# First half's output projection moved between the second half's receptances and values in a two-layer RWKV-7 and S5 trunk

## The chip, the cores and the metric

One core of a Trainium2 chip runs the whole kernel. The metric is the time of one execution in device microseconds (us): the median of three runs before the change is 2767.67 us (2766.5 to 2772.65). A difference under 0.2%, some 5.5 us, is called no change.

## The reference

The input x is 1024 steps of 1024 channels. Layer 0 is RWKV-7 time mixing, layer 1 a diagonal state-space mixer (S5), each followed by a squared-ReLU MLP, and after each of the four parts comes `x <- LayerNorm(sqrt(2) * x + f(x))`. The change lies in layer 0:

```python
r = xr @ wr; k = xk @ wk; v = xv @ wv          # xr, xk, xv: x mixed with its last step
w_pre = w0 + tanh(xw @ w1) @ w2                # decay
a = sigmoid(a0 + (xa @ a1) @ a2); g = sigmoid(xg @ g1) @ g2
def step(state, inp):                          # 16 heads of 64, 1024 steps in sequence
    sa = einsum('bhvk,bhk->bhv', state, a_t)
    state = state * w_t + sa * b_t + v_t * k_t
    return state, einsum('bhvk,bhk->bhv', state, r_t)
o = group_norm(o) * lnx_g + lnx_b + bonus
return (o * g) @ wo
```

## The kernel before

All operands are float32. A dense product of 128 output channels by 512 steps is made of three TensorE matmuls for each 128 input channels: both operands are split into a high part (rounded by ScalarE, `whi`, `oAh`) and the rest (subtracted by VectorE, `wlo`, `oAl`), and high x high, high x low and low x high are summed in one PSUM tile `d` (`mm3`, `dense`, L175). So a projection of 1024 channels on half the sequence is 8 tiles of 24 matmuls.

The sequence is worked in two halves of 512 steps. `rwkv_proj(H)` computes receptances, keys, values, rates and gates of half H and stores them in DRAM. The recurrence then runs in 8 **units** m = 0 to 7, each 256 steps by 8 heads: units 0 to 3 belong to the first half, units 4 to 7 to the second. Even and odd units carry the states of different heads. For a unit, `elem` forms the decayed vectors, `amat` (L550 on) the chunk matrices (`AT`: products within 64-step chunks), `invert` the triangular inverses `XT` by some 60 short VectorE instructions in sequence, and `chain` walks four 64-step chunks: products pR, pX, pU, pO of 8 heads (L672, L677, L682, L691 and L693), each waiting for a copy of the one before. `gnorm` normalises and writes the unit's y to DRAM.

`core()` lists these pieces with a priority (`rank`): a scheduler places the instructions of all engines by it, lowest number first where they are ready. What it makes is a fixed order for each engine, each worked strictly in that order; DMAs are issued by SyncE's queue in such an order too. The dense products have high numbers and fill the time that the chains leave. `rwkv_proj(1)` is listed at unit 3 (`PB`), all of it with rank 100000. At unit 5 (`W0B`) come `wo(0)`, the output projection of the first half (rank 99000), and its LayerNorm (rank -1). `wo` loads y, makes its operands, and adds each product to sqrt(2) x in a tile `hA`. The MLP's products follow: `up` (relu, square, split into `qbuf`) and `down`.

Two pools matter. Tag "xs" holds 8 tiles: the mixed input's x of the second half until the last mix (that for the values) has read it, then `hA`. Tag "q" has one buffer, which is held in turn by `stash`, by the chunk matrices `AT2` of units 1, 3 and 5 (all other units have their own tile `AT`), and then by the MLP's `qbuf`:

```python
if D.m in (1, 3, 5):
    at = ap.tile(shp, F32, tag="q", name="AT2", bufs=1)
else:
    at = kp.tile(shp, F32, tag="AT", name="AT", bufs=1)
```

Of the kernel before, what the change touches and what calls it, by code (L numbers as in the profile page):

```python
# [8 lines left out]
F32 = mybir.dt.float32  # L9
# [9 lines left out]
HT = 512  # L19
# [13 lines left out]
TB = 2  # L33
LN8R = 400000
MIXR = 100
W0B = 5
ARB = 5
GB = (2, 3, 4)
GV = True
# [31 lines left out]
def trunk(ctx, tc, A):  # L71
# [13 lines left out]
    @contextmanager  # L85
    def rank(base):

        keep = tc.cur_priority
        tc.cur_priority = base
        yield  # L90
        tc.cur_priority = keep
# [137 lines left out]
    def rwkv_proj(H):  # L229
# [196 lines left out]
        else:  # L426
# [8 lines left out]
            for n in range(KT):  # L435
                square("wr", "r", xm, n)


        xv = list(mixes(3))
        for cb in range(4):  # L440
# [260 lines left out]
    def gnorm(D, half):  # L701

        def gwt(shape, name):
            if D.m < 4:
                return tp.tile(shape, F32, tag="la", name=name, bufs=2)
            return kp.tile(shape, F32, tag=GWT, name=name, bufs=1)

        q, o, vsa = D.q, D.o[half], D.vsa[half]
        t0 = D.t0 + half * 128
        og = o.rearrange("p c i v -> p (c i) v")  # L710
        bc = [128, 8, 64]
        sm = kp.tile([128, 8], F32, tag="sm", name="sm", bufs=2)
        V.tensor_reduce(sm, og, axis=AX.X, op=ALU.add)
        V.tensor_scalar(sm, sm, 1.0 / 64, None, op0=ALU.mult)
        (G if GNG[0] else V).tensor_sub(og, og, sm.unsqueeze(2).broadcast_to(bc))
        sq = gwt([128, 8, 64], "osq")
        S.activation(sq, og, AF.Square)
        vr = kp.tile([128, 8], F32, tag="sm", name="vr", bufs=2)
        V.tensor_reduce(vr, sq, axis=AX.X, op=ALU.add)
        V.tensor_scalar(vr, vr, 1.0 / 64, GN_EPS, op0=ALU.mult, op1=ALU.add)  # L720
        G.tensor_tensor(vr, vr, mhalf[:, 0:8], op=ALU.pow)
        (G if GNG[1] else V).tensor_mul(og, og, vr.unsqueeze(2).broadcast_to(bc))
        vt = gwt([128, 2, NP, 64], "vt")
        if half == 0:
            D.lg = kp.tile([128, 2, 256], F32, tag="lg", name="lg", bufs=LGB)
            for h in range(2):
                for j in range(2):
                    fs = slice(q * 512 + h * 256, q * 512 + h * 256 + 256)
                    SP.dma_start(D.lg[64 * (1 - h) : 64 * (1 - h) + 64, j], A["lnx"][j : j + 1, fs].broadcast_to([64, 256]))
        lg = D.lg  # L730
        for h in range(2):
            hs = slice(64 * (1 - h), 64 * (1 - h) + 64)
            G.tensor_mul(vt[hs], vsa[hs, :, h],
                         D.bo[hs, 2 * half : 2 * half + 2].unsqueeze(3).broadcast_to([64, 2, NP, 64]))
        o2 = o.rearrange("p c i v -> p c (i v)")
        v2 = vt.rearrange("p c i v -> p c (i v)")
        G.tensor_add(v2, v2, lg[:, 1:2].broadcast_to([128, 2, 256]))
        G.tensor_mul(o2, o2, lg[:, 0:1].broadcast_to([128, 2, 256]))
        G.tensor_add(o, o, vt)
        rows = slice(q * 512, q * 512 + 512)  # L740
        gt = kp.tile([128, NP, 128], F32, tag="gt", name="gt", bufs=GTB)
        SP.dma_start(gt, scr["g"][rows, t0 : t0 + 128].rearrange("(i p) t -> p i t", p=128))

        p = pc.tile([128, HT], F32, tag="c", name="py").rearrange("p (u h c l) -> p u h c l", u=2, h=2, c=2)
        for u in range(2):
            for c in range(2):
                PE.transpose(p[:, u, :, c], o[:, c, 2 * u : 2 * u + 2].rearrange("p i v -> p (i v)"), ident)
        V.tensor_mul(gt, gt, p.rearrange("p u h c l -> p (u h) (c l)"))
        SP.dma_start(scr["y"][rows, t0 : t0 + 128].rearrange("(i p) t -> p i t", p=128), gt)

    def run(gen):
        for _ in gen:
            pass

    first_out = []

    def core():

        pg = rwkv_proj(0)
        next(pg)  # L760
        bulk.clear()
        with rank(3000):
            cur = elem(0)
        with rank(5000):
            amat(cur)
            invert(cur)
        with rank(100000):
            run(pg)
        last = None
        for m in range(8):  # L770
            if m == PB:
                with rank(100000):
                    run(rwkv_proj(1))
            if m == W0B:

                with rank(WO0R):
                    first_out.append(wo(0))
                with rank(LN1R):
                    first_out.append(layer_norm(first_out[0], 0, 0))
            base = m * 10000  # L780
            with rank(base + RK[0]):
                kbtrans(cur)
            nxt = None
            if m < 7:
                with rank(base + RK[1]):
                    nxt = elem(m + 1)
            if last and m in GB:
                with rank(base + RK[2]):
                    gnorm(last, 1)
            with rank(base):  # L790
                chain(cur, 0)
            if last and m not in GB:
                with rank(base + RK[2]):
                    gnorm(last, 1)
            if nxt and m < 6:
                with rank(base + RK[3]):
                    amat(nxt)
            with rank(base + RK[4]):
                chain(cur, 1)
            with rank(base + RK[5]):  # L800
                gnorm(cur, 0)
            if nxt:
                with rank(base + RK[6]):
                    if m == 6:
                        amat(nxt)
                    invert(nxt)
            last, cur = cur, nxt
        with rank(base + 8000):
            gnorm(last, 1)


    def htile(H):
# [2 lines left out]
        return sp.tile([128, HT], F32, tag="hB", name="hB", bufs=8)  # L815

    def layer_norm(h, gi, H, split_out=True):
        g, b = f"g{gi}", f"b{gi}"

        def lt(name, tag="la"):  # L820
            return tp.tile([128, HT], F32, tag=tag, name=name, bufs=2)

        def plt(name):
            return pl.tile([128, HT], F32, tag="l", name=name)

        a, b2 = lt("sa"), lt("sb")
        G.tensor_add(a, h[0], h[1])
        G.tensor_add(a, a, h[2])
        V.tensor_add(b2, h[3], h[4])
        for t in h[5:7]:  # L830
            V.tensor_add(b2, b2, t)
        V.tensor_add(a, a, b2)
        pm = plt("pm")
        PE.matmul(pm, ones_c, a, start=True, stop=False)
        PE.matmul(pm, ones_c, h[7], start=False, stop=True)
        for t in h:
            V.tensor_sub(t, t, pm)
        sa = [lt("sq0"), lt("sq1")]
        for k, t in enumerate(h):
            if k < 2:  # L840
                S.activation(sa[k], t, AF.Square)
            else:
                q = lt("sq", "m")
                S.activation(q, t, AF.Square)
                (G if k % 2 else V).tensor_add(sa[k % 2], sa[k % 2], q)
        pq = plt("pq")
        for t in range(4):
            for j in range(2):
                PE.matmul(pq[:, t : t + 1], sa[j][:, t * 128 : (t + 1) * 128], ones_c[:, 0:1], start=j == 0, stop=j == 1)  # L849
        rs = tp.tile([128, 4], F32, tag="rs", name="rs")  # L850
        V.tensor_scalar(rs, pq[:, 0:4], LN_EPS, None, op0=ALU.add)
        G.tensor_tensor(rs, rs, mhalf[:, 0:4], op=ALU.pow)
        rb = lt("rb").rearrange("p (t n) -> p t n", t=4)
        S.copy(rb, rs.unsqueeze(2).broadcast_to([128, 4, 128]))
        pr = plt("pr")
        for t in range(4):
            PE.transpose(pr[:, t * 128 : (t + 1) * 128], rb[:, t], ident)
        ops = []
        for k, t in enumerate(h):
            V.tensor_mul(t, t, pr)  # L860
            S.activation(t, t, AF.Identity, bias=vec(b, k), scale=vec(g, k))
            if split_out:
                ops.append(operand(t, H, G if k in LNG else V))
        return ops

    def last_norm(h, gi, c):
# [49 lines left out]
            ys.append(operand(y, H))  # L916
        return ys

    def wo(H):
        t0 = H * HT  # L920
        ys = yload(H)
        hs = []
        for n in range(KT):
            p = psd()
            dense(p, wload(A["wo"][n], KT, 128), ys)
            h = htile(H)
            SP.dma_start(h, A["xT"][n * 128 : (n + 1) * 128, t0 : t0 + HT])
            V.scalar_tensor_tensor(h, h, ALPHA, p, op0=ALU.mult, op1=ALU.add)
            hs.append(h)
        return hs  # L930
# [309 lines left out]
        for k in range(KT):  # L1240
            SP.dma_start(A["out"][k * 128 : (k + 1) * 128, H * HT : (H + 1) * HT], h[k])

    core()
    kctx.close()
    sp = ctx.enter_context(tc.tile_pool(name="sp", bufs=1))

# [1 line left out]
    bw = sp.tile([128, 4, 32, 2], F32, name="bw")  # L1248
    qbuf = ap.tile([128, 2 * KB2, 2, HT], F32R, tag="q", name="qbuf", bufs=1)
    tc.cur_priority = 200000  # L1250
    hA, xo = first_out
    ma = mlp(0, 0, hA, xo)
    for _ in range(INS1):
        next(ma)
# [110 lines left out]
```

## Time and profile before

| | |
|---|---|
| median of three runs | 2767.67 us |
| the profiled execution | 2764.91 us, of which its span 2763.2 us |
| busy share of the span: TensorE (PE), VectorE (DVE), ScalarE (ACT), GpSimd (POOL) | 94%, 68%, 40%, 26% |
| mean granted TensorE clock | 0.958 of full speed |
| moved by DMA | 318.63 MB, mean 115 GB/s |

The profile gives, for each engine, how long it worked, and, for idle time before an instruction, what ended it. A matmul's recorded time overlaps its neighbours', so the rate is read from the distance between starts. A float32 product of the chains shows as two records for each matmul. PEclk is the mean granted clock of TensorE as a share of 2.4 GHz; its two levels are 1.2 and 2.4 GHz.

### The profile page before, as it was taken

The numbers are of one execution on the slowest core, as the hardware profiler recorded it, in microseconds if no ns is written. First come the engines' busy times: TensorE is split into PE (matmuls) and PEld (weight loads), VectorE is DVE, ScalarE is ACT, GpSimd is POOL, SyncE is SP. The second block draws the span as 40 slices with busy tenths as digits, with TensorE's granted clock in tenths as the row PEclk, the third lists the DMA queues.
The fourth block names the chain that finished last, engine by engine and source line by source line (L and its number), as shares of the span: only waits on it lengthen the run. The fifth ranks groups of instructions, "written<-read, shape, count | busy, mean of one in ns | idle before, by whom it ended". The sixth has DMA issues, their size and how long they took to land.

```text
span 2763.2 us, 43707 instructions
## 1 busy us (share of the span) xinstructions
PE 2604.9 (94%) x16582; PEld 2096.5 (76%) x16582; DVE 1884.5 (68%) x3242; ACT 1109.5 (40%) x1952; POOL 719.6 (26%) x601
## 2 busy tenths in 40 slices
PE   7889989889899999989999999999999999999997
PEld 5779767678677877767776788778778887788886
DVE  7487788587787777998658554574765546755556
ACT  5445454544443333334432332344323323533333
POOL 5331664450352303233122001121220101210101
PEclk9989969889889999999999999999999999999998
DMA  3543443344222323555332633223343322333333
GB/s 115 184 147 112 139 162 102 109 138 135 77 81 81 100 85 124 154 145 159 96 122 99 203 96 98 89 88 102 117 160 112 99 96 84 119 96 97 98 95 100
DMA packets 200083, 318.63 MB, mean 115 GB/s; under 512 B 19520, under 2 KB 73920, under 8 KB 199872
## 3 DMA queue, kind: packets, MB, share of 16 engines
q1 hardware_dynamic: 199872, 315.83, 36.6%
q8 instruction: 131, 2.15, 0.3%
q14 instruction: 80, 0.66, 0.1%
HBM read 265.42 MB, written 50.33 MB: 114 GB/s over the span
## 4 chain that ended last, share of the span: by engine, by line
PE 45%; DVE 5%; issue 2%; POOL 1%; DMA 1%; ACT 0%; ACTq 0%; DVEq 0%; POOLq 0%
PE d L175 40%; PE py L1219 1%; PE py L1224 1%; DVE wlo L147 1%; PE pu L152 1%; DVE t L1187 1%; PE pbu L1175 1%; DVE hA L960 0%; DVE hB L960 0%; DVE t L1185 0%; POOL rl L944 0%; PE pq L849 0%; DMA wraw<-in_mw_dram 0%; PE pu L1164 0%; DVE qbuf L147 0%
## 5 line engine op out<-in xcount | busy, mean ns | idle before, releaser
L147 DVE TENSOR_TENSOR wlo<-wraw,whi 128x512 fp32r<-128x512 f32 x720 | 535.6, 745 | 443.7 <-ACT whi L146 424.8
L146 ACT CAST whi<-wraw 128x512 fp32r<-128x512 f32 x720 | 445.7, 620 | 975.4 <-PE d L175 637.2
L175 PE MATMUL d<-qbuf,whi 128*128 128x512 f32 (+1 forms) x2112 | 655.6, 393 | 20.9 <-DVE hA L960 9.4
L175 PEld LDWEIGHTS d<-qbuf,whi 128*128 128x128 f32 x2112 | 390.3, 190 | 117.7 <-DVE hA L960 17.0
L944 POOL TENSOR_TENSOR rl<-rl 128x512 f32<-128x512 f32 x128 | 158.6, 1239 | 1058.4 <-ACT rl L943 1018.1
L175 PE MATMUL d<-qbuf,wlo 128*128 128x512 f32 (+1 forms) x1056 | 409.3, 390 | 8.2 <-DVE wlo L147 8.0
L175 PE MATMUL d<-oAh,whi 128*128 128x512 f32 (+1 forms) x960 | 387.8, 408 | 9.6 <-ACT ev L404 7.2
L175 PE MATMUL d<-oAh,wlo 128*128 128x512 f32 (+1 forms) x960 | 387.2, 406 | 5.3 <-DVE wlo L147 5.1
L175 PE MATMUL d<-oAl,whi 128*128 128x512 f32 (+1 forms) x960 | 385.5, 404 | 1.4 <-DVE oAl L147 1.4
L175 PE MATMUL d<-oBh,wlo 128*128 128x512 f32 x704 | 278.3, 396 | 1.4 <-DVE wlo L147 1.4
L175 PE MATMUL d<-oBh,whi 128*128 128x512 f32 x704 | 278.8, 396 | 0.0
L175 PE MATMUL d<-oBl,whi 128*128 128x512 f32 x704 | 276.1, 392 | 0.0
L175 PEld LDWEIGHTS d<-qbuf,wlo 128*128 128x128 f32 x1056 | 200.6, 190 | 52.8 <-DVE wlo L147 11.7
L175 PEld LDWEIGHTS d<-oAh,whi 128*128 128x128 f32 (+1 forms) x960 | 185.1, 194 | 54.2 <-ACT ev L404 9.2
L175 PEld LDWEIGHTS d<-oAh,wlo 128*128 128x128 f32 (+1 forms) x960 | 184.9, 193 | 49.1 <-DVE wlo L147 8.6
L175 PEld LDWEIGHTS d<-oAl,whi 128*128 128x128 f32 (+1 forms) x960 | 184.8, 193 | 40.6 <-DVE oAl L147 2.1
L960 DVE TENSOR_TENSOR hB<-hB,d 128x512 f32<-128x512 f32 (+1 forms) x256 | 165.2, 650 | 68.9 <-PE d L175 65.8
L960 DVE TENSOR_TENSOR hA<-hA,d 128x512 f32<-128x512 f32 x240 | 162.5, 683 | 54.5 <-PE d L175 52.5
L175 PEld LDWEIGHTS d<-oBh,wlo 128*128 128x128 f32 x704 | 132.5, 188 | 33.8 <-DVE wlo L147 2.0
L175 PEld LDWEIGHTS d<-oBl,whi 128*128 128x128 f32 x704 | 132.7, 188 | 29.4 <-issue 0.5
L175 PEld LDWEIGHTS d<-oBh,whi 128*128 128x128 f32 x704 | 132.7, 189 | 29.1 <-issue 1.5
L147 DVE TENSOR_TENSOR qbuf<-rl,qbuf 128x512 fp32r<-128x512 f32 x128 | 99.0, 774 | 70.3 <-ACT qbuf L146 69.8
(371 smaller groups left out, 3877.1 us busy)
## 6 DMA issues: line engine op xcount, KB each, us to landing
wraw<-in_mw_dram SPq DMA_DIRECT2D x520, 256.0 KB, 2.7
wraw<-in_glu_dram SPq DMA_DIRECT2D x64, 256.0 KB, 2.6
wraw<-in_wk_dram SPq DMA_DIRECT2D x32, 256.0 KB, 3.1
wraw<-in_wr_dram SPq DMA_DIRECT2D x32, 256.0 KB, 3.1
wraw<-in_wv_dram SPq DMA_DIRECT2D x32, 256.0 KB, 3.4
yl<-s_y SPq DMA_DIRECT2D x32, 256.0 KB, 3.1
wraw<-in_wo_dram SPq DMA_DIRECT2D x32, 256.0 KB, 2.8
tb<-tB SPq DMA_DIRECT2D x16, 512.0 KB, 4.9
```

The lines of the kernel that those rows point to most:

```text
L146: S.copy(hi, src)
L147: (e or V).tensor_sub(lo, src, hi.bitcast(F32))
L152: PE.matmul(out, x, idt, start=True, stop=True)
L175: bulk.append((PE.matmul(p, w, x, **kw).ins, x.shape[-1]))
L944: G.tensor_mul(r, r, r)
L960: V.tensor_add(z, z, p)
L1175: PE.matmul(p[qs, g2, ri], tb[:, g2, ri, qs], u[:, 2 * g2 + par], start=True, stop=True)
L1187: e.tensor_mul(t2[:, :, ri], x[:, :, 1 - ri], bw[:, l, g0:g1, ri : ri + 1].broadcast_to([128, g1 - g0, n]))
L1219: PE.matmul(p[64 * j : 64 * j + 64, g2], ug[f][:, 2 * g2 + par], tv[:, par, g2], start=g2 == 0, stop=False, skip_group_check=True)
L1224: PE.matmul(p[64 * j : 64 * j + 64, g2], hb[qs, 4 * f + g2, ri, 0:NSC], tcm[qs, g2, ri], start=False, stop=ri == 1, skip_group_check=True)
```

## The change

`rwkv_proj(1)` stops after the receptances. `wo(0)` is listed there, at unit 4, and puts its sums in a new tile `pre` of tag "q", which thus lies between the chunk matrices of unit 3 and those of unit 5. Then the values of the second half are listed, then the LayerNorm, cut in `ln_stats` and `ln_apply`; the latter writes its result to fresh `hA` tiles of tag "xs".

```diff
             for n in range(KT):
                 square("wr", "r", xm, n)
+        if H == 1:
+            yield
         xv = list(mixes(3))
...
             if m == PB:
+                pg = rwkv_proj(1)
                 with rank(100000):
-                    run(rwkv_proj(1))
-            if m == W0B:
-
-                with rank(WO0R):
-                    first_out.append(wo(0))
-                with rank(LN1R):
-                    first_out.append(layer_norm(first_out[0], 0, 0))
+                    next(pg)
...
+            if m == 4:
+
+                pre = ap.tile([128, KT, HT], F32, tag="q", name="pre", bufs=1)
+                with rank(WO0R):
+                    hA = wo(0, pre)
+                with rank(100000):
+                    run(pg)
+                with rank(LNR):
+                    xo = ln_apply(hA, ln_stats(hA), 0, 0, fresh=True)
...
+    def ln_apply(h, pr, gi, H, split_out=True, fresh=False):
+        g, b = f"g{gi}", f"b{gi}"
         ops = []
         for k, t in enumerate(h):
             V.tensor_mul(t, t, pr)
-            S.activation(t, t, AF.Identity, bias=vec(b, k), scale=vec(g, k))
+            h[k] = htile(H) if fresh else t
+            S.activation(h[k], t, AF.Identity, bias=vec(b, k), scale=vec(g, k))
...
-    def wo(H):
+    def wo(H, room=None):
...
-            h = htile(H)
+            h = htile(H) if room is None else room[:, n]
```

What that does to the order of instructions is seen at three places. First, SyncE's queue at the end of the receptances (`in_wr`, `in_wo`, `in_wv` are the weights of receptances, output projection and values; `hA` and `pre` receive x; `yl` is a row of y). Before:

```order
L163 DMA wraw<-in_wv_dram 128x512
L927 DMA hA<-in_xT_dram 128x512
L485 DMA ldr<-s_r 128x2x256
L927 DMA hA<-in_xT_dram 128x512 x2
L163 DMA wraw<-in_wv_dram 128x512
L927 DMA hA<-in_xT_dram 128x512
L485 DMA ldsg<-s_sg 128x2x256
L485 DMA lda<-s_a 128x2x256
L927 DMA hA<-in_xT_dram 128x512
L163 DMA wraw<-in_wv_dram 128x512
```

and after it:

```order
L938 DMA pre<-in_xT_dram 128x512 x7
L487 DMA ldk<-s_k 128x2x256
L938 DMA pre<-in_xT_dram 128x512
L751 DMA s_y<-gt 128x4x128
L163 DMA wraw<-in_wo_dram 128x512
L365 DMA s_r<-ev 128x512
L163 DMA wraw<-in_wo_dram 128x512
```

The loads of x for the output projection stood between the weights of the values; now they stand together ahead of the first weights of the output projection, which follow the receptances directly.

Second, VectorE's order around the chunk matrices of unit 5, which are `AT_6976` before and `AT_7453` after (an `AT` with no number is an even unit's). Before, they are written during the values' projection:

```order
L570 TENSOR_TENSOR AT_6976<-pA,amask 128x2x256
L608 TENSOR_TENSOR x_6530<-xa,x_6530 128x96
L570 TENSOR_TENSOR AT_6976<-pA,amask 128x2x256
L610 TENSOR_TENSOR x_6530<-x_6530 128x8x12
L608 TENSOR_TENSOR x_6530<-xa,x_6530 128x84
```

and now:

```order
L857 TENSOR_SCALAR rs<-pq 128x4
L147 TENSOR_TENSOR wlo<-wraw,whi 128x512
L870 TENSOR_TENSOR pre<-pre,pr 128x512 x8
L147 TENSOR_TENSOR wlo<-wraw,whi 128x512
L680 COPY vsa<-pX 64x256
L572 TENSOR_TENSOR AT_7453<-pA,amask 128x2x256 x2
L147 TENSOR_TENSOR wlo<-wraw,whi 128x512 x2
L687 TENSOR_TENSOR st<-pU,st 128x256
```

They come behind the LayerNorm's last multiplications, in the time of unit 4's chain, and no longer among the steps of unit 4's inverse.

Third, TensorE's order at the start of unit 5's chain (`pT` are transposes for that chain, `pv` the last products of its inverse, `pm` the LayerNorm's mean, `pb` and `pss` products of unit 6's `elem`). Before:

```order
L580 MATMUL pT<-ident,KB 128x128 x4
L175 MATMUL d<-oAh,whi 128x512
L175 MATMUL d<-oAl,whi 128x512
L175 MATMUL d<-oAh,wlo 128x512
L175 MATMUL d<-oAh,whi 128x512
L175 MATMUL d<-oAl,whi 128x512
L175 MATMUL d<-oAh,wlo 128x512
L672 MATMUL pR<-vsa,AT_6976 64x64 x8
L544 MATMUL pb<-rksel,kf 64x1 x2
L834 MATMUL pm<-sa,ones_c 128x512
L544 MATMUL pb<-rksel,kf 64x1 x12
L835 MATMUL pm<-hA,ones_c 128x512
```

and now:

```order
L749 MATMUL py<-ident,o 128x2x64 x4
L582 MATMUL pT<-ident,KB 128x128 x4
L623 MATMUL pv_7717<-x_7644,AT_7453 32x32 x32
L582 MATMUL pT<-ident,KB 128x128 x8
L631 MATMUL pv_7717<-XT,x_7644 32x32 x32
L582 MATMUL pT<-ident,KB 128x128 x4
L546 MATMUL pb<-rksel,kf 64x1 x7
L674 MATMUL pR<-vsa,AT_7453 64x64 x8
L546 MATMUL pb<-rksel,kf 64x1 x9
L509 MATMUL pss<-hsel,sq 128x2 x4
L679 MATMUL pX<-o,XT 64x64 x8
```

Unit 5's inverse stood some 70 dense matmuls ahead of its chain and now ends right before it. The LayerNorm's products are gone from here. From this `py` to the end of unit 5's chain no dense matmul stands in the new order; before, the first 96 of the MLP (its four `up` tiles) stood in that chain, and now they are ahead of it.

## Rows read from the trace of the kernel before

**Rows 1.** The page, parts 1 and 4: busy time; the chain that ended last, by engine.

```profile
PE 2604.9 (94%) x16582; PEld 2096.5 (76%) x16582; DVE 1884.5 (68%) x3242; ACT 1109.5 (40%) x1952; POOL 719.6 (26%) x601
...
PE 45%; DVE 5%; issue 2%; POOL 1%; DMA 1%; ACT 0%; ACTq 0%; DVEq 0%; POOLq 0%
```

**Rows 2.** Stretches: length, busy us of PE, PEld, DVE, ACT, POOL; granted clock, DMA share, GB/s.

```profile
579.00:741.00 162.00, 145.27 (x1352) 126.70 (x1352) 126.24 (x261) 69.64 (x126) 44.75 (x37) 0.89 0.38 120
587.00:619.00 32.00, 27.00 (x168) 25.34 (x168) 30.28 (x53) 15.34 (x28) 18.43 (x15) 0.68 0.42 133
741.00:776.00 35.00, 25.40 (x285) 21.20 (x284) 30.79 (x47) 16.39 (x31) 24.65 (x21) 0.66 0.26 80
776.00:813.00 37.00, 36.22 (x313) 28.64 (x311) 31.99 (x59) 20.72 (x41) 17.24 (x15) 1.00 0.20 65
813.00:862.00 49.00, 43.85 (x272) 34.81 (x268) 48.15 (x98) 16.57 (x29) 23.13 (x16) 0.90 0.30 92
```

**Rows 3.** Timeline, TensorE, end of the receptances: start, us, instruction, idle before it and releaser.

```profile
578.58 0.39 PE L175 MATMUL d<-oAh,wlo 128*128 128x512 f32 x1
...
587.29 0.58 PE L175 MATMUL d<-whi,oAh 128*128 128x256 f32 x1 [1.30 <-ACT oAh L146]
```

**Rows 4.** Timeline, SyncE's queue, loads between the values' weights.

```profile
590.08 3.70 SPq L927 DMA_DIRECT2D hA<-in_xT_dram  x2
595.96 0.33 SPq L163 DMA_DIRECT2D wraw<-in_wv_dram  x1
```

**Rows 5.** Timeline, TensorE: rate of the 256-wide (values) and 512-wide dense matmuls.

```profile
641.84 0.28 PE L175 MATMUL d<-whi,oAl 128*128 128x256 f32 x1
641.96 0.28 PE L175 MATMUL d<-whi,oAh 128*128 128x256 f32 x1
...
693.38 0.39 PE L175 MATMUL d<-oAh,wlo 128*128 128x512 f32 x1
693.60 0.39 PE L175 MATMUL d<-oAh,whi 128*128 128x512 f32 x1
```

**Rows 6.** Timeline, TensorE: unit 5's chain and the LayerNorm.

```profile
741.11 0.69 PE L672 MATMUL pR<-vsa,AT 128*64 128x64 f32 x16
...
741.93 1.12 PE L834 MATMUL pm<-sa,ones_c 128*128 128x512 f32 x2
...
776.08 0.73 PE L175 MATMUL d<-oAh,whi 128*128 128x512 f32 x2
...
812.44 0.69 PE L693 MATMUL pO<-vsa,AT 128*64 128x64 f32 x16
```

**Rows 7.** Tile hA in the LayerNorm: ns min/median/max, first and last start.

```profile
L837 DVE TENSOR_TENSOR hA<-hA,pm x8: 681/682/683, 745.4 to 749.5; 128x512 f32<-128x512 f32 x8
L860 DVE TENSOR_TENSOR hA<-hA,pr x8: 679/680/681, 771.3 to 775.5; 128x512 f32<-128x512 f32 x8
L861 ACT ACTIVATE hA<-hA,pv x8: 801/812/816, 772.1 to 779.3; 128x512 f32<-128x512 f32 x8
```

**Rows 8.** Timeline, VectorE: unit 5's chunk matrices (first, last of 8) and inverse (L600 to L615).

```profile
625.36 0.68 DVE L570 TENSOR_TENSOR AT<-pA,amask 128x512 f32<-128x512 f32 x1
...
641.19 0.69 DVE L570 TENSOR_TENSOR AT<-pA,amask 128x512 f32<-128x512 f32 x1
...
657.75 2.07 DVE L600 STREAM_TRANSPOSE xa<-x 128x1024 f32<-128x1024 f32 x1 [3.79 <-ACT x L599]
...
709.01 1.25 DVE L615 STREAM_TRANSPOSE XT<-x 128x1024 f32<-128x1024 f32 x1
```

**Rows 9.** Timeline, TensorE: chunks of units 2 and 3 with hardly a dense matmul.

```profile
395.91 1.12 PE L672 MATMUL pR<-vsa,AT 128*64 128x64 f32 x16
...
427.61 0.69 PE L672 MATMUL pR<-vsa,AT 128*64 128x64 f32 x16
...
496.53 0.69 PE L672 MATMUL pR<-vsa,AT 128*64 128x64 f32 x6
...
507.17 0.69 PE L672 MATMUL pR<-vsa,AT 128*64 128x64 f32 x16
```

More of the change, by code (lines that the diff above doesn't have):

```diff
@@ L35 @@
 MIXR = 100
-W0B = 5
+LNR = -1
 ARB = 5
@@ L753, in run @@
             pass
-    first_out = []
     def core():
@@ L809, in core @@
             gnorm(last, 1)
+        return hA, xo
     def htile(H):
@@ L817, in layer_norm, with ln_stats @@
     def layer_norm(h, gi, H, split_out=True):
-        g, b = f"g{gi}", f"b{gi}"
+        return ln_apply(h, ln_stats(h), gi, H, split_out)
+    def ln_stats(h):
         def lt(name, tag="la"):
@@ L857, in layer_norm @@
             PE.transpose(pr[:, t * 128 : (t + 1) * 128], rb[:, t], ident)
+        return pr
+    def ln_apply(h, pr, gi, H, split_out=True, fresh=False):
+        g, b = f"g{gi}", f"b{gi}"
         ops = []
@@ L860, in layer_norm @@
             V.tensor_mul(t, t, pr)
-            S.activation(t, t, AF.Identity, bias=vec(b, k), scale=vec(g, k))
+            h[k] = htile(H) if fresh else t
+            S.activation(h[k], t, AF.Identity, bias=vec(b, k), scale=vec(g, k))
             if split_out:
-                ops.append(operand(t, H, G if k in LNG else V))
+                ops.append(operand(h[k], H, G if k in LNG else V))
         return ops
@@ L1241, in store @@
             SP.dma_start(A["out"][k * 128 : (k + 1) * 128, H * HT : (H + 1) * HT], h[k])
-    core()
+    hA, xo = core()
     kctx.close()
@@ L1250, in trunk @@
     tc.cur_priority = 200000
-    hA, xo = first_out
     ma = mlp(0, 0, hA, xo)
```

## The prediction

> **What bounds the kernel now.** I read the page first. TensorE is busy for 94% of the span, and the chain that ended last runs over it for 45% and over VectorE for 5% [rows 1]: the kernel is a stream of dense matmuls, so a change is worth what it takes from the places where that stream stands still or runs at the low clock. The table of stretches shows such places near the change [rows 2]. Between the receptances' last matmul at 578.6 us and the values' first at 587.3 there is no dense work [rows 3]. From 587 to 619 TensorE is booked busy for 27.0 of 32 us, but at a granted clock of 0.68, and VectorE for 30.3 [rows 2]. From 741 to 776 the granted clock is 0.66 and the LayerNorm of the first half keeps the MLP back; its first matmul comes at 776.1 [rows 2, 6]. Then TensorE works 36.2 of 37 us until unit 5's chain ends at 813.1 [rows 2, 6].
>
> The end of unit 5's chain is the point that I forecast. There the tile of tag "q" comes free for `qbuf`, and in both orders the same dense matmuls stand ahead of it: receptances, values, output projection and the MLP's first 96. VectorE has the same work behind it there too, but for its place. After it, TensorE is booked for 43.9 of 49 us and VectorE for 48.2 [rows 2], so that nothing hides a shift: what is gained or lost at 813.1 should stand at the end.
>
> **The change part by part.** *Dense work that moves.* The 192 matmuls of the output projection change places with the 384 of the values: 0.23 us each (693.60 - 693.38 and their like) against 0.12 us [rows 5]; their sum is the same. The MLP's four `up` tiles, 96 matmuls, now stand ahead of unit 5's chain, 96 x 0.23 = 22 us, and leave it by as much.
>
> *The wait and the ramp at 579 to 619.* Unit 2's rows of y lie in DRAM when the receptances end, so that the first four of eight steps of three tiles, 36 x 0.23 = 8.3 us, can fill the 8.7 us from 578.6 to 587.3. In the ramp the values' first two tiles and part of the third, 116 matmuls by count, need 116 x 0.12 = 14 us and take 32. Two things hold them: VectorE, busy for 95%, and SyncE's queue, where loads of x into `hA` wait for tiles of tag "xs" (590.1, two of them in 3.7 us) and the weights behind them go out at 596.0 [rows 4]. The second cause goes, since `pre` waits for no mix; the first stays in part, as inverse 4 now runs under the output projection. I take 16 us for wait and ramp together; the bounds are 8 (the wait alone) and 24 (the ramp down to its matmuls).
>
> *The LayerNorm's products* now stand in the stream ahead of unit 5: two for the mean of two records, 2 x 1.12 us [rows 6], and small ones that I put at 4 us: 6 us (3 to 8). VectorE's share, eight subtractions and eight multiplications of 0.68 [rows 7] and about as many other steps, some 18 us, moves too: VectorE had 126 us to do in the 162 us before unit 5's chain [rows 2]. With 18 more and the `up` weights' eight splits at 0.69, 150 us, at the 95% of the ramp that is 158: it does not bind.
>
> By TensorE's stream unit 5's chain thus starts at 741.1 + 22 + 6 - 16 = 753 us.
>
> *The wait that is added.* Unit 5's chunk matrices need `pre` to be read to its end. Before, they were written from 625.4 to 641.9, the inverse ran from 657.8 to 710.3, and the chain came at 741.1 [rows 6, 8], with 30 us in hand. Now the path is serial: output projection (44 us of matmuls and some 8 of unit 5's `elem`) from 579 to 631; ramp of the values, 24 us, with the mean's product at its end, 655; LayerNorm to its last activation, 38 us in the trace (741.9 to 780.1) [rows 6, 7], less 9 for what unit 5's chain took from it in between, 684; eight matrix products, 12 us (5.5 by their durations, 16.5 as they lay) [rows 8], 696; a wait for the copies of 4 (3.8 in its row), 700; inverse, 52.5 us in the trace [rows 8], less 4 as the steps of the projection no longer stand between, 748.5; TensorE's last products of the inverse, 8, to 757. What is queued behind: unit 4's first copies stand behind eight activations of 0.81 us [rows 7] on ScalarE, 6.5 us, on a chain that ends before 757 even so. In SyncE's queue the eight loads into `pre` wait for unit 3's chain, and y and the projection's weights behind them; the receptances' weights are ahead: nothing (0 to 3). GpSimd's part falls where it has room, nothing. I take the later of the two, 757 (745 to 770).
>
> *Unit 5's chain without dense work.* It took 72.0 us, from 741.1 to 813.1 [rows 6], with the LayerNorm's VectorE work and 22 us of dense matmuls in it. The nearest rows are chunks with hardly any dense work: two of unit 2 in 31.7 us, 15.9 each, beside heavy VectorE work, and one of unit 3 in 10.6 [rows 9]. The mean, 13.2, for four, less 3 since the last chunk ends at its output: 50 us (42 to 62). It ends at 757 + 50 = 807 us, against 813.1: **6 us earlier**.
>
> These chunks run at the low level: a product of a chunk is 1.12 us there and 0.69 at the full one [rows 9]; at full clock the four chunks' five products would take 4 x 5 x 0.43 = 8.6 us less, and 50 would be 41. The stretch from 741 to 776, also without dense work, was granted 0.66, that is about a third of it at 2.4 GHz [rows 2]. The Trainium skill ("TensorE: Matmul & The Clock Gate", Part 1) says that TensorE is at 1.2 GHz by default and that only sustained activity releases 2.4. By that rule the chain has the low level throughout and the 50 stand, as their rows are at that level; by the third of 741 to 776 they would be 3 us less. I keep 50.
>
> *Sum.* The profiled execution took 2764.9 us, its span 2763.2 and 1.7 around it, and lies 2.8 us under the median of the runs. 2764.9 - 6 = 2759 for such an execution, **2762 us** for the median.
>
> **The rivals.** *A: the inverse comes late (slower).* The serial path is made of steps that I shortened by what stood in their way. With the rows as they are, LayerNorm 38, matrices 16.5, inverse 52.5, it ends at 757 + 9 + 4.5 + 4 = 774, and a chain of 50 us ends at 824: +11 us, 2779. For it speaks that VectorE has even more to do in that stretch; against it, that the steps were stretched by the work that is moved away. It decides as soon as unit 5's chain starts after 763. The LayerNorm's GpSimd work also comes to lie beside VectorE's splits now.
>
> *B: the hole only moves (no change).* The 35 us hole under the LayerNorm and the hole under the bare chain are of one size: before, 72.0 - 22 = 50 us of unit 5's chain were without dense work, and 50 us are so now. If the ramp keeps its length under VectorE's load (gain 8 in place of 16) and the path of 757 becomes 761 to 763, the chain ends within 5 us of 813: 2765 to 2768.
>
> *C: more is gained.* If the ramp gives up all its 24 us, the LayerNorm is through early and the chunks run at 10.6 as unit 3's did, the chain starts at 748 and ends at 787 to 790: some 24 us less, 2744. Against it stands VectorE's load.
>
> That the change does not do what it says can be left out: the order shows each piece moved.
>
> **How the numbers follow.** I give the forecast 0.45, A 0.28, B 0.17, C 0.10. A measurement tells 0.2%, some 5.5 us, from no change; of my own case about 0.33 lies beyond that, and 0.12 within, as 6 us is hardly over it. Faster: 0.33 + 0.10 = 0.43; the same: 0.12 + 0.17 = 0.29; slower: 0.28. The range goes from C's 2744 to a little over A's, 2783; the corners of all bounds together (745 + 42, 770 + 62) reach further, and I leave them out. Cases of both signs hold most of the chance: my own case alone spans 2752 to 2767.
>
> **What would show it.** In the new profile the stretch from 579 to 587 holds matmuls of the output projection; the ramp of the values, some 45 us later, takes 20 to 24 us and not 32; the LayerNorm's `pre` steps lie beside dense matmuls at a clock near 1. Unit 5's first pR stands at about 757, with nothing dense from there to its last pO at about 807, a granted clock of 0.5 to 0.7 there, and after it all is as before by 6 us. I am wrong if that last pO comes after 813, and A is the reason if VectorE's inverse of unit 5 ends after 755; I am wrong in size if the chunks take over 14 us each with VectorE idle in them, or if the difference at 813 is not the difference at the end.

## The result

The change is slower: 2776.65 us (median of 20 runs, 2771.16 to 2786.26) against 2767.76 (20 runs, 2756.45 to 2777.38), a ratio of 1.0034, 95% interval 1.0025 to 1.0044, some 9 us. The forecast was 2762, and faster, with a range from 2744 to 2783 and a chance of 0.28 for slower. A second set of the change (e18) gave 1.0039 (1.0025 to 1.0054).

The page's busy times and chain after it, parts 1 and 4, hardly differ from [rows 1]: a loss of 0.34% doesn't show in shares.

```profile
PE 2609.1 (94%) x16582; PEld 2101.8 (76%) x16582; DVE 1883.5 (68%) x3242; ACT 1107.1 (40%) x1952; POOL 721.4 (26%) x601
...
PE 46%; DVE 5%; issue 1%; DMA 1%; ACT 1%; POOL 1%; ACTq 0%; DVEq 0%; POOLq 0%
```

To compare like with like I count from the end of the receptances' last tile but one, up to which both orders agree: 568.1 us before, 571.4 after. The 3.3 us between are scatter of two executions. "From that tile" means this below. Every kernel here works the same number of dense matmuls (records `d<-...`), so the n-th of them after that tile also serves as a mark of progress; the two profiled executions of the change, its own and e18's, agree within 2.4 us at every such mark. Stretches of the kernel before, up to both products, output projection and values, through (741.2), the MLP's first matmul (776.1), the first `down` matmul (816.6) and the end of the sixteenth `down` tile; columns as in [rows 2]:

```profile
568.10:741.20 173.10, 153.70 (x1403) 133.03 (x1403) 134.04 (x269) 71.95 (x130) 51.84 (x41) 0.90 0.39 121
741.20:776.10 34.90, 25.30 (x285) 21.13 (x285) 30.69 (x46) 16.49 (x31) 24.75 (x21) 0.66 0.25 80
776.10:816.60 40.50, 37.96 (x321) 30.11 (x321) 35.25 (x71) 23.07 (x45) 17.14 (x15) 0.99 0.21 66
816.60:868.10 51.50, 47.98 (x323) 37.50 (x322) 50.29 (x93) 18.38 (x31) 24.17 (x18) 0.91 0.30 93
```

The same of the change, up to both products through (723.5), the four `up` tiles through (757.5), unit 5's first pR (767.6), the first `down` matmul, the sixteenth `down` tile; then the stretch that [rows 2] has for the ramp:

```profile
571.40:723.50 152.10, 140.65 (x1137) 119.95 (x1136) 119.22 (x211) 74.95 (x132) 49.10 (x38) 0.94 0.38 114
723.50:757.50 34.00, 30.91 (x237) 24.25 (x235) 32.31 (x80) 12.16 (x26) 14.97 (x12) 0.95 0.29 86
757.50:767.60 10.10, 7.00 (x163) 5.79 (x162) 7.92 (x15) 7.36 (x13) 2.62 (x3) 0.83 0.41 120
767.60:825.40 57.80, 41.15 (x471) 35.80 (x471) 43.73 (x84) 17.14 (x37) 28.72 (x25) 0.62 0.19 58
825.40:880.30 54.90, 50.90 (x411) 40.43 (x410) 49.56 (x91) 20.55 (x37) 25.80 (x18) 0.91 0.29 87
587.00:619.00 32.00, 31.49 (x180) 25.18 (x180) 27.62 (x52) 15.75 (x27) 14.03 (x11) 1.00 0.43 137
```

TensorE's busy time multiplied by the granted clock is an estimate of the time that its work would take at the full clock; a stretch's length less that is what it lost. Before: 173.1 - 153.7 x 0.90 = 34.8, then 18.2 and 2.9. After: 152.1 - 140.65 x 0.94 = 19.9, then 4.6, 4.3 and 32.3. So up to the point where both products are through **14.9 us are gained** (34.8 - 19.9), and behind it **20.1 are lost** (41.2 against 21.1): 8.9 of them ahead of unit 5's first pR (4.6 + 4.3), and 11.2 under its chain (32.3, where the kernel before lost 21.1 in all under its chain and LayerNorm). To the first `down` matmul the change takes 254.0 us and the kernel before 248.5: 5.5 more. To the sixteenth `down` tile it is 308.9 against 300.0: 8.9. That this is also the difference of the medians is in part chance: at later marks the change is 3.7 to 17.2 us behind, and 13.2 at the last dense matmul of the two profiled executions.

Timeline of TensorE after: the projection's first matmul, the first after its wait, the LayerNorm's mean, the last `up` matmul, unit 5's first and last product, the first `down` matmul:

```profile
577.81 0.48 PE L175 MATMUL d<-oAh,whi 128*128 128x512 f32 x1
580.61 0.80 PE L175 MATMUL d<-oAl,whi 128*128 128x512 f32 x1 [2.33 <-DVE oAl L147]
...
667.03 1.02 PE L840 MATMUL pm<-sa,ones_c 128*128 128x512 f32 x2
...
757.14 0.39 PE L175 MATMUL d<-oAh,wlo 128*128 128x512 f32 x1
...
767.62 1.12 PE L674 MATMUL pR<-vsa,AT 128*64 128x64 f32 x16
...
822.31 0.69 PE L695 MATMUL pO<-vsa,AT 128*64 128x64 f32 x16
...
825.43 0.73 PE L175 MATMUL d<-qbuf,whi 128*128 128x512 f32 x2
```

Timeline of VectorE after: the last operand of the mean (L939), the first subtraction (L843), unit 5's chunk matrices (first and last), its inverse (L602 to L617):

```profile
649.38 0.68 DVE L939 SCALAR_TENSOR_TENSOR pre<-pre,d 128x512 f32<-128x512 f32 x1
...
668.95 0.69 DVE L843 TENSOR_TENSOR pre<-pre,pm 128x512 f32<-128x512 f32 x1 [4.10 <-PE pm L841]
...
697.19 1.29 DVE L572 TENSOR_TENSOR AT<-pA,amask 128x512 f32<-128x512 f32 x2 [1.10 <-ACT hA L872]
...
713.28 0.69 DVE L572 TENSOR_TENSOR AT<-pA,amask 128x512 f32<-128x512 f32 x1 [0.78 <-PE pA L569]
...
715.46 2.11 DVE L602 STREAM_TRANSPOSE xa<-x 128x1024 f32<-128x1024 f32 x1
...
759.79 1.23 DVE L617 STREAM_TRANSPOSE XT<-x 128x1024 f32<-128x1024 f32 x1
```

The matrices stand right behind the LayerNorm's last activation (697.19, released by hA), and the chain behind the inverse, as rival A had it. Whether that wait is what costs is for the experiments.

### The profile page after: what moved, and what is told of

It reads as the page before. It is cut to its first block, busy times and chain, and to the rows that moved or that the text cites. A ratio compares the mean times of both kernels' runs of the same rounds, so it can differ in the third digit from the quotient of the medians.

```text
span 2779.2 us, 43722 instructions
## 1 busy us (share of the span) xinstructions
PE 2609.1 (94%) x16582; PEld 2101.8 (76%) x16582; DVE 1883.5 (68%) x3242; ACT 1107.1 (40%) x1952; POOL 721.4 (26%) x601
## 4 chain that ended last, share of the span: by engine, by line
PE 46%; DVE 5%; issue 1%; DMA 1%; ACT 1%; POOL 1%; ACTq 0%; DVEq 0%; POOLq 0%
PE d L175 41%; PE py L1230 1%; PE py L1235 1%; DMA wraw<-in_mw_dram 1%; DVE wlo L147 1%; PE pu L152 1%; PE pbu L1186 1%; POOL rl L955 1%; DVE t L1198 0%; DVE hA L971 0%; DVE t L1196 0%; DVE hB L971 0%; PE pq L855 0%; PE pu L1175 0%; PE pu L154 0%
## 6 DMA issues: line engine op xcount, KB each, us to landing
wraw<-in_mw_dram SPq DMA_DIRECT2D x520, 256.0 KB, 2.7
wraw<-in_glu_dram SPq DMA_DIRECT2D x64, 256.0 KB, 2.6
wraw<-in_wk_dram SPq DMA_DIRECT2D x32, 256.0 KB, 3.0
wraw<-in_wr_dram SPq DMA_DIRECT2D x32, 256.0 KB, 2.9
wraw<-in_wv_dram SPq DMA_DIRECT2D x32, 256.0 KB, 3.2
yl<-s_y SPq DMA_DIRECT2D x32, 256.0 KB, 3.3
wraw<-in_wo_dram SPq DMA_DIRECT2D x32, 256.0 KB, 2.9
```

## The experiments

Ratios are to the kernel before, measured beside each, with 95% intervals. Start, end and `down` are us from that tile: unit 5's first pR, its last pO, the first `down` matmul in one profiled execution each. In the kernels with halves (e3 to e5, e14 to e17, explained below) that tile itself ends later: the 337 dense matmuls up to it take 140.5 to 144.8 us there and 129.7 to 135.0 in all others, and the units are further on by then (unit 4's inverse ends 69.4 us behind it in e5, 85.6 in the change). So their three columns are to be compared among themselves.

| kernel | us | ratio | start | end | down |
|---|---|---|---|---|---|
| before | 2767.76 | 1 | 173.0 | 245.0 | 248.5 |
| change | 2776.65 | 1.0034 (1.0025-1.0044) | 196.2 | 251.6 | 254.0 |
| e1 | 2779.05 | 1.0060 (1.0044-1.0076) | 197.6 | 256.4 | 258.4 |
| e6 | 2777.55 | 1.0034 (1.0021-1.0046) | 196.7 | 254.5 | 256.7 |
| e12 | 2771.14 | 1.0028 (1.0009-1.0047) | 199.7 | 253.7 | 256.0 |
| e13 | 2773.22 | 1.0026 (1.0008-1.0044) | 195.4 | 247.1 | 249.7 |
| e2 | 2778.51 | 1.0051 (1.0038-1.0064) | 200.8 | 252.6 | 254.5 |
| e8 | 2766.27 | 0.9998 (0.9984-1.0011) | 190.6 | 244.0 | 246.3 |
| e9 | 2774.40 | 1.0033 (1.0021-1.0046) | 192.8 | 246.4 | 248.3 |
| e10 | 2769.88 | 1.0012 (1.0000-1.0025) | 190.8 | 246.2 | 248.1 |
| e7 | 2789.16 | 1.0063 (1.0038-1.0088) | 198.7 | 262.2 | 263.8 |
| e11 | 2775.14 | 1.0034 (1.0022-1.0045) | 196.5 | 239.4 | 241.3 |
| e4 | 2770.73 | 1.0014 (1.0002-1.0025) | 151.2 | 224.4 | 247.6 |
| e5 | 2768.11 | 1.0007 (0.9993-1.0021) | 182.7 | 245.8 | 208.9 |
| e3 | 2757.02 | 0.9966 (0.9954-0.9978) | 178.7 | 234.6 | 206.5 |
| e14 | 2751.30 | 0.9956 (0.9938-0.9974) | 183.2 | 245.5 | 212.2 |
| e15 | 2766.67 | 1.0002 (0.9983-1.0020) | 177.9 | 246.8 | 205.2 |
| e16 | 2770.61 | 1.0007 (0.9992-1.0021) | 183.1 | 235.9 | 235.8 |
| e17 | 2749.24 | 0.9934 (0.9920-0.9948) | 181.9 | 244.0 | 211.3 |
| e18 (the change again) | 2778.85 | 1.0039 (1.0025-1.0054) | 197.2 | 253.5 | 255.5 |

**The waits on unit 5's path (e1, e6, e12, e13).** e1 lets the subtractions write to hA, so that `pre` is free after them:

```
-            V.tensor_sub(t, t, pm)
+            h[k] = htile(0) if fresh else t
+            V.tensor_sub(h[k], t, pm)
```

> The changed kernel with one edit: the LayerNorm's eight subtractions of the mean write to tiles hA, so that the tile pre is free after them (673.8 us in the trace of the change) and not after the last of eight activations (697.2). Theory (unit 5's chain starts late because its matrices wait for pre): the matrices are written from about 674 to 690, VectorE ends unit 5's inverse by about 740, the chain starts when the MLP's four up tiles are through, at 755 to 760 in place of 767.6, and the time is 8 to 11 us less than that of the change: 2766 to 2769 us. Rival (VectorE's load and the longer projection hold everything, and the wait is only a symptom): the inverse keeps its end within 5 us, the chain starts after 763, and the time stays at 2773 to 2778.

The inverse was through at 749.6, 13 us earlier from that tile (176.6 against 189.6), and the chain started no earlier. Unit 5's inverse products had been placed ahead of 41 `up` matmuls (the expectation of e6 says 49), and TensorE waited 3.8 us before them; e6 takes that away with an ordering edge:

```
+    for ins in held:
+        tc.add_manual_dep(ins, ups[2], NoSync, reason="hold")
```

> The edit of e1, with unit 5's inverse products held on TensorE until the MLP's third up tile is through (in e1 they were placed ahead of 49 up matmuls, and TensorE stood before them until 748.0 us). Theory (the stretch under the chain is the loss, and the wait on pre only sets where it begins): the up tiles end at about 756, the chain starts at 757 to 760, some 8 us earlier than in the change, and the time is 4 to 9 us under the change, 2768 to 2773, hardly under the kernel before. Rival (the wait is no cause at all): chain start after 764, 2775 to 2780.

The start did not move either (196.7), and the time is the change's (1.0034): the rival. e12 took another wait: the mean's operands are ready at 650.1 and it runs at 667.0 only, since unit 4's inverse holds the one PSUM tile of tag "l".

```
-        pm = plt("pm")
+        pm = pc.tile([128, HT], F32, tag="c", name="pm")
```

> The changed kernel with one edit: the sum for the LayerNorm's mean of the first half stands in a PSUM tile of tag c (two of them, the chain's) and not of tag l (one, which unit 4's inverse holds until about 666 us). Theory (that wait made the path long): the mean is taken at 650 to 652 us in place of 667, the subtractions follow at once, unit 5's inverse is through on VectorE by 745 to 750, its chain starts at 755 to 759 as forecast, and the time is 5 to 10 us under the change, 0 to 0.2% above the kernel before or level with it. Rival (VectorE's load sets the start whatever is early): the mean is early, the chain starts after 764, and the time is within 3 us of the change.

> e12 and e1 together: early mean, and pre free after the subtractions. Theory (two waits in a row, each hides the other): unit 5's matrices are written from about 658, its inverse is through by 725 to 735, and its chain starts when the up tiles are through, 748 to 753; 9 to 15 us under the change, level with the kernel before or up to 0.25% under it. Rival (after the mean, VectorE's load is the limit): within 3 us of e12.

The mean came at 642.7 to 646.5 and the time stayed: by the ratios e12 is 1.7 us under the change and e13 2.2, so the rivals hold. In e12 the earlier mean hardly moved the path: unit 5's first matrix came 123.2 us from that tile, 125.8 in the change. e13 is the clearest of the four, in VectorE's and TensorE's timelines (end of unit 5's inverse; the last `up` matmul; first pR):

```profile
725.61 1.24 DVE L617 STREAM_TRANSPOSE XT<-x 128x1024 f32<-128x1024 f32 x1
```

```profile
752.55 0.39 PE L175 MATMUL d<-oAh,wlo 128*128 128x512 f32 x1
...
761.05 0.69 PE L674 MATMUL pR<-vsa,AT 128*64 128x64 f32 x16 [0.19 <-ACT kbt L584]
```

With its tile at 565.6, the inverse ends 161.3 us from it, 28 earlier than in the change (189.6); the chain starts at 195.4, where it started at 196.2. Neither wait is what sets the start. Between the last `up` matmul and that pR TensorE has unit 4's last products and the transposes for unit 5 to do, and waits for only 2.2 of the 8.1 us.

**VectorE's load (e2, e8, e9, e10).** e2 put 12 subtractions of the projection on GpSimd:

> The changed kernel with 12 of the 24 subtractions that make the low parts of the first output projection's weights and of y put on GpSimd (every second weights tile, every second y tile): 12 x 0.68 = 8 us off VectorE between 580 and 645 us. Theory (the projection ended at 645 and not at 631 because VectorE was full): its last matmul comes 5 to 8 us earlier, the whole serial path with it, unit 5's chain starts at 760 to 763, and the time is 4 to 7 us less than that of the change, 2769 to 2773. Rival (TensorE or the loads of y set the projection's end): it ends at 645 within 2 us, or later as GpSimd's subtraction takes 1.3 to 1.6 us, and the time is 2775 to 2781.

They took twice as long there, and the projection ended 83.1 us from that tile, not 73.8, as the rival allowed for, and the time is no better (1.0051). GpSimd's groups from 560 to 660 us:

```profile
L147 POOL TENSOR_TENSOR wlo<-wraw,whi 128x512 fp32r<-128x512 f32 x8 | 10.7, 1342 | 2.1 <-ACT whi L146 2.1
L147 POOL TENSOR_TENSOR oAl<-yl,oAh 128x512 fp32r<-128x512 f32 x4 | 5.5, 1388 | 3.3 <-ACT oAh L146 3.3
```

So e8, e9 and e10 leave subtractions out (`lo = hi` in `wload` for the weights named). They leave out a part of the product too, so they weigh VectorE's load and are no versions to use:

> The changed kernel with one thing left out: the low parts of the first output projection's weights, whose place in the matmuls is taken by the high parts (16 subtractions, 16 x 0.68 = 11 us of VectorE between 565 and 645 us; TensorE does the same matmuls). Theory (VectorE is full under the projection, 52 of 58 us, and sets its end): the projection ends 8 to 11 us earlier against the receptances' last-but-one tile, unit 5's chain starts 6 to 11 us earlier, and the time is 5 to 10 us under the change, 2767 to 2772. Rival (loads of y, TensorE): the projection ends within 3 us of the change's, and the time stays.

> The changed kernel with the low parts of the second half's value weights and of the MLP's first two up tiles left out in the same way (16 subtractions of the values, 4 of the up tiles, 20 x 0.68 = 13.6 us of VectorE between 640 and 757 us). Theory (from 700 to 758 VectorE, busy for 50.6 of 58 us, holds the up tiles and unit 5's inverse both): unit 5's chain starts 6 to 12 us earlier, and the time is 5 to 12 us under the change, 2765 to 2772. Rival (the serial path through pre, and not VectorE's load, sets the start): 3 us or less.

> The edit of e1 and the omission of e9 together. Theory (wait and load are two holds on one engine: in e1 the earlier inverse only pushed the up tiles' weights back): together 12 to 20 us under the change, with unit 5's chain at 748 to 755, more than e1 (none) and e9 added up. Rival (the load alone): the time of e9 within 3 us.

e8's projection was as long as the change's (74.3 against 73.8 from that tile): its length is not the doing of these 11 us of VectorE, and there the rival is right. But unit 4's inverse, which shares VectorE with it, ended 68.7 us from that tile (636.7) and not 85.6 (657.0), the chain started 5.6 us earlier, and the ratio fell from 1.0034 to 0.9998. e9 takes more off VectorE, later, and gains nothing in the runs (its profiled start is 3.4 us earlier). e10 gained 6 us where 12 to 20 were expected; it is 0.22% under the change (the intervals just meet) and 0.48% under e1, whose edit it holds. So VectorE's load counts under the projection; behind it, it counts once the matrices come early (e10 against e1, each by its own ratio) and not by itself (e9).

**Inside the chain (e7, e11).** e7 sets filler matmuls behind unit 5's products:

```
+    mm = PE.matmul(full[0][:, 256:512], xo0[0][:, 0:128], xo0[0][:, 0:256], ...)
```

> The changed kernel with 104 extra matmuls (256 columns, results in the unused half of the chain's own PSUM tiles, read by nobody) set behind unit 5's products, 8, 6 and 16 at a time: 104 x 0.12 = 12.5 us at the full clock, where TensorE stands idle for 16.6 us from 768 to 825. They add work and take none away. Theory (some 23 us of that stretch are TensorE's own instructions at the low level of its clock): the granted clock there rises from 0.6 to 0.8 or more, the chain's products shorten, and the chain takes 45 to 52 us in place of 55.4: 3 to 10 us under the change. Rival (the chain is set by the hops over ScalarE and VectorE): the chain takes 55 to 65 us, the time is that of the change or up to 8 us more.

Its stretches, the chain and the part in which the clock was up:

```profile
785.00:815.00 30.00, 25.59 (x291) 22.51 (x291) 21.65 (x38) 8.35 (x17) 9.99 (x10) 0.92 0.18 53
766.00:830.00 64.00, 53.16 (x571) 46.93 (x570) 46.97 (x92) 15.11 (x33) 27.61 (x23) 0.74 0.17 53
```

The granted clock rose to 0.74 (0.92 in the middle), and the chain took 63.4 us: the rival. The filler stands between the chain's products and is itself 12.5 us of work at the full clock, so the run shows that filler does not pay; what the chain would take at a higher clock without it stays open. e11 holds unit 6's matrices until the chain is through, by the same kind of edge as e6:

> The changed kernel with the 32 products of unit 6's chunk matrices held on TensorE until unit 5's chain is through (in the change they and their eight VectorE steps stand between its products). Theory (the chain took 55 and not 50 us because unit 6's work stands between its hops on TensorE and VectorE, at the low clock): the chain takes 42 to 48 us, the first down matmul comes 7 to 13 us earlier, unit 6 comes some 20 us later beside dense work, and the time is 4 to 10 us under the change, 2767 to 2773. Rival (the hops alone set the chain): it takes 53 us or more, and the time is that of the change or more.

The chain shrank as the theory said, from 55.4 to 42.9 us, and the first `down` matmul came 12.7 us earlier; the time stayed, against the theory. The gain is lost much later. At the 1600th dense matmul after that tile e11 is still 16.0 us ahead of the change, at the 2100th 16.9, and at the 2400th 1.5. The stretch from the 2100th to the 2420th takes 104.5 us in e11 and 89.2 in the change:

```profile
1240.10:1344.60 104.50, 94.77 (x493) 71.73 (x492) 93.21 (x140) 49.63 (x81) 42.27 (x29) 0.95 0.56 156
```

```profile
1262.30:1351.50 89.20, 83.09 (x367) 65.02 (x367) 66.15 (x93) 40.29 (x67) 22.48 (x17) 0.96 0.41 124
```

VectorE is busy for 93.21 us there in e11 and 66.15 in the change: 41.5 of them, against 7.5, are steps that build tables of the S5 layer (`tw`, `ca`, `bp`, `bb`). These begin 576 us from that tile in e11 and 544 in the change, after unit 7's chain, which ends at 538.3 and 504.3. So the units that e11 made late seem to take back what its chain gave; no run moves the one without the other.

**Dense work under the chain (e3 to e5, e14 to e18).** The tile of tag "q" is cut in two halves, by chunks:

```
-            at = ap.tile(shp, F32, tag="q", name="AT2", bufs=1)
+            D.at = [(ap.tile([128, 2, 2, NP, 2, L], F32, tag=f"q{x}", ...), 2 * x, 2) for x in range(2)]
...
-                qt = qbuf[:, n + KB2 * (b % 2)]
+                qt = qbuf[b % 2][:, n]
```

> The kernel before, with the tile of tag q cut in two halves alone. Theory (before, the four up tiles already stood beside unit 5's chain, so that a half that comes free earlier lets little more work in): within 4 us of the kernel before, 2764 to 2772. Rival (the halves are worth the same in either order, and e3 shows them and not the order): 8 us or more under the kernel before, 2760 or less.

> The changed kernel with the tile of tag q in halves, and without the edit of e1: the LayerNorm's activations still free pre. Theory now (e1 moved unit 5's matrices up by 15 to 20 us and gave nothing, so that the loss is the stretch under unit 5's chain, which holds some 18 us of TensorE work in 57 us): the halves alone bring most of what e3 brought, 10 to 17 us off the change, 2760 to 2767 us, with the first down matmuls at about 795. Rival (the late matrices and the halves each hold the end, and only both together help): 4 us off at most, 2773 to 2777.

> The edit of e1, and the tile of tag q cut in two halves of 8 KB, chunks 0 and 1 of a unit's matrices in one, 2 and 3 in the other: the MLP's first two up tiles can be written when chunk 1 of unit 5 is through, and 48 matmuls of its down projection and some more stand beside chunks 2 and 3. Theory (what is left after e1 is the bare chain of unit 5, 50 to 55 us with hardly any dense work): 11 us of matmuls find room in it, and the time is 8 to 13 us less than that of e1: 2754 to 2760, faster than the kernel before. Rival (the chain's chunks grow by what is put between them, or VectorE binds): the time is that of e1 within 3 us.

> e5 and e12 together: the tile of tag q in halves, and the mean's own PSUM tile. In e5's trace the mean stood at 650 us already. Theory (the halves' gain in e5 is partly that early mean, which is there anyway): within 4 us of e5. Rival (the wait on tag l still cost in e5): 5 us or more under e5.

> e3 and e12 together: halves, pre free after the subtractions, and the mean's own PSUM tile. Theory: e3's mean stood at 656 us; a few us earlier gives at most 3 us more than e3, 0.3 to 0.45% under the kernel before. Rival: without its order of instructions e3's gain is lost, and the time is within 0.2% of the kernel before.

In the old order the halves gain nothing (e4): unit 5's chain is through 20.6 us earlier from that tile, but the first `down` matmul comes 0.9 earlier, and that tile 8.7 later. In the new one they gain 0.3% alone (e5, 7 us where 10 to 17 were expected), and with one more edit 0.7 to 0.8% (e3, 26 us under e1 where 8 to 13 were expected, and e14, 14 us under e5 where at most 4 were), or 0.3% with both (e15, a miss). These edits also re-deal the order of instructions; I take no meaning from e15 against e3. What the halves gain was settled by e16, which is e14 with its first 48 `down` matmuls held until the chain is through, with its references on one chip:

> e14 with the MLP's first 48 down matmuls held on TensorE until unit 5's chain is through; all before stays as in e14. Theory (the loss is the bare chain of unit 5): 8 to 13 us over e14, 2759 to 2766 us, with the chain some 10 us shorter than in e14, as less stands in it. Rival (the halves gain by the earlier units alone): within 4 us of e14.

> The kernel of e14 unchanged, beside e16 and e18 on one chip: 0.3 to 0.6% under the kernel before, 2748 to 2757 us. If it comes out above 2760, e14's gain was of that chip alone.

> The change itself, beside e16 and e17 on one chip: 0.25 to 0.45% over the kernel before, 2772 to 2780 us.

The stretches up to unit 5's first pR, to its end, and to the sixteenth `down` tile; e16, then e17:

```profile
584.20:767.30 183.10, 167.88 (x1491) 141.23 (x1489) 151.58 (x296) 95.57 (x176) 60.86 (x47) 0.96 0.35 106
767.30:820.10 52.80, 41.68 (x477) 36.87 (x477) 41.35 (x74) 17.56 (x37) 31.05 (x26) 0.55 0.23 71
820.10:876.80 56.70, 47.98 (x401) 38.00 (x402) 50.59 (x101) 21.11 (x39) 21.12 (x17) 0.94 0.28 85
```

```profile
575.30:757.20 181.90, 166.45 (x1490) 140.08 (x1488) 151.06 (x295) 94.74 (x176) 61.06 (x47) 0.97 0.35 106
757.20:819.30 62.10, 54.41 (x548) 44.99 (x548) 51.70 (x96) 21.45 (x44) 31.10 (x26) 0.75 0.24 77
819.30:843.70 24.40, 22.92 (x136) 18.85 (x135) 24.10 (x54) 11.24 (x21) 10.07 (x7) 0.93 0.38 119
```

Up to the chain the two are alike. In e16 it lies bare (1 dense matmul in it, 72 in e17) and loses 52.8 - 41.68 x 0.55 = 29.9 us, and 11.6 more up to the sixteenth tile; in e17 it is 21.3 and 3.1: 17 us less. The runs say 2770.61 against 2749.24: **21 us**, more than was expected, and at the last dense matmul e16 is 22.4 us behind e17 from that tile. Behind the chain the two also differ in the order of TensorE's instructions in the second layer, so a few of the 21 us may come from there. Of the 29.6 us between e18 (2778.85) and e17, these 21 are the cover of the chain. The other 8 lie between e18 and e16, which differ by the halves and by the mean's PSUM tile; they were not taken apart. The kernel of e14 and e17, 0.44% and 0.66% under the one before in its two sets, is the version that beats both.

## Why the prediction was wrong

- *The gain* was right where it was counted: 16 forecast for wait and ramp, 14.9 found up to the point where both products are through. The ramp's 116 matmuls took 22.2 us (645.0 to 667.2), as said, and 31.2 before. The 8.7 us were not filled cleanly: TensorE waited 2.33 us for y's low parts, and 579 to 587 was granted 0.57. But the gain did not last: at unit 5's first pR 6.0 of it are left (34.8 lost before, 28.8 after).
- *The start of unit 5's chain* is the step that failed first. It was forecast at 757 and came at 767.6, 764.3 without the scatter of 3.3. Both of its sums came out at about 764. By the path's terms, the projection was mis-sized: through at 645.2, 73.8 us from that tile, where the forecast had 631, which is 62.9 from it; its 52 us from 579 became 67.4 from its first matmul, with the receptances' last ones among them. The matrices took 16.8 (697.2 to 714.0) and not 12, the LayerNorm 30.2 and not 29, the inverse 45.5 and not 48.5. By TensorE's stream, "741.1 + 22 + 6 - 16 = 753" had the added work nearly right (29.1 us at the full clock by the stretches above, where 22 + 6 was said), but counted on 16 where 6.0 were left: 741.1 + 29.1 - 6.0 = 764.2. It put at nothing what is lost under the `up` tiles (4.6) and between the last of them and the first pR (4.3). So "I take the later of the two" is not shown to be at fault: with both sums at 764, shortening the path alone should leave the start where it was, and it did (e1, e6, e13). What they share is VectorE, of which the forecast said "it does not bind". e8 shows otherwise: with 11 us less on it the start comes 5.6 us earlier and the time is back at that of the kernel before. How the load delays each of the two is argued, not shown: that an earlier inverse pushes the stream back fits e1 and e6, whose `up` tiles end 194.1 and 194.7 us from that tile in place of 186.2, and not e13 (187.3).
- *The chain* is the second, in its size: 50 us forecast (42 to 62), 55.4 measured; the four chunks took 17.8, 14.4, 15.3 and 7.9. e11 says why: unit 6's matrices stand between its hops, 42.9 without them. The rows behind the 50 were not at the low level throughout, as the forecast says of them: 395.9 to 427.6 was granted 0.62 and 496.5 to 507.2 0.60, much as the chain itself (0.62), so the 50 were kept for a wrong reason. 7.3 at the start and 5.4 in the chain make 12.7, and the forecast of 6 us less becomes 6.6 more at the last pO (819.7 against 813.1).
- *"what is gained or lost at 813.1 should stand at the end"*: 5.5 at the first `down` matmul, 8.9 at the sixteenth tile and in the medians, 3.7 to 17.2 at the marks behind it. The 3.4 between the first two were not tried. e11 shows that a gain there need not stand: 12.7 us at the first `down` matmul, and none at the end.
- *The rivals*: by its sign (inverse through after 755, chain after 763) and its price (+11 against 9) A came true, but not by its mechanism, the wait on `pre`, whose removal gave nothing. The mechanism is nearer to B's, with a size that B denied: the hole moved and grew, from 21.1 us lost to 41.2, of which 32.3 lie under the chain. B called the holes "of one size" because it set 50 us of chain without dense work before against 50 us now; but before, the LayerNorm's work and 96 dense matmuls stood beside that chain, and the us lost differ. e16 against e17 prices a bare chain, in the kernel with halves.
- *The clock*: 0.62 under the chain, in the forecast's 0.5 to 0.7; some quarter of it at 2.4 GHz, so neither the low level throughout nor the third of 741 to 776. The Trainium skill ("TensorE: Matmul & The Clock Gate", Part 1) says that only sustained activity releases 2.4 GHz; e7 agrees: with filler the granted clock went from 0.62 to 0.74. It changed no time for the better.

## What to carry to other kernels

Dense work that is moved ahead of a serial chain is missing beside the chain: price that stretch by length less busy time times granted clock, before and after, and not by lengths. When one wait is taken away and the start doesn't move, a second bound stands at the same time: look for the engine that both share, and for what can stand in the hole. Follow a local gain to the end, since a later stage can take it back (e11). Here what could stand in the hole was a tile cut in halves, so that the next stage's work could begin while the chain still ran.

## What was not expected of the hardware

A subtraction of 128x512 took 1.34 to 1.39 us on GpSimd (e2) where VectorE takes 0.68, within what e2's rival allowed for. Raising TensorE's granted clock by filler (e7) shortened a group of 16 products from 1.12 to 0.69 us, and the chain of such groups, with the filler between them, was longer all the same: 63.4 against 55.4 us.
